# A batched matrix product bound by its transfers: taking out a 64 KB store beside the first loads

## The chip, the core and the metric

The kernel runs on one core of one Trainium2 chip. The time is device microseconds of one execution; medians over several executions are given. The profile is one execution, recorded by the hardware profiler; its "span" runs from the first to the last instruction and is about 2 us shorter than the time.

## The reference

```python
batch, m, k, n = 16, 512, 512, 512
# a: (16, 512, 512) float32 as (batch, k, m);  b: (16, 512, 512) float32 as (batch, k, n)
out = np.matmul(a.transpose(0, 2, 1), b).astype(np.float32)
```

Each of the 16 batches reads 1 MB of a and 1 MB of b and writes 1 MB, some 50.3 MB in all.

## The kernel before

SyncE issues all loads, then all stores. VectorE casts a and b to bf16, TensorE multiplies, ScalarE copies the results from PSUM into one output tile per batch.

```python
NL = 3      # load buffers
NB = 2      # bf16 buffers and PSUM pairs
H = MO // 2
...
o_ts = [pool.tile([P, MO, N], f32, name=f"o{j}") for j in range(batch)]
...
def load(i):
    j = i % NL
    if i >= NL:
        nc.sync.wait_ge(s_acast, i - NL + 2)
    nc.sync.dma_start(a_ts[j][:], a_v[i]).then_inc(s_a[j], 16)
    nc.sync.dma_start(b_ts[j][:], b_v[i]).then_inc(s_b[j], 16)

def store(i):
    if i == 0:
        nc.sync.wait_ge(s_w, 16)
    nc.sync.wait_ge(s_ev1, i + 1)
    nc.sync.dma_start(out_v[i], o_ts[i][:]).then_inc(s_o, 16)

for i in range(batch):
    load(i)
for i in range(batch):
    store(i)
...
nc.gpsimd.memset(o_ts[0][:, 0, 0:P], 0.0).then_inc(s_z, 1)
nc.scalar.wait_ge(s_z, 1)
nc.scalar.dma_start(out_v[0][:, 0, 0:P], o_ts[0][:, 0, 0:P]).then_inc(s_w, 16)
nc.scalar.wait_ge(s_w, 16)
for i in range(batch):
    for h in range(H):
        nc.scalar.wait_ge(s_mm, H * i + h + 1)
        nc.scalar.copy(
            out=o_ts[i][:, 2 * h:2 * h + 2, :], in_=ps_ts[(i % NB) * H + h][:]
        ).then_inc(s_ev1 if h else s_ev0, 1)
```

The four lines with s_z and s_w ahead of ScalarE's loop, and SyncE's wait for s_w in store(0), are the subject. They write 64 KB of zeros, 128 rows of 512 B, into a corner of the output that the first real store overwrites later.

Of the kernel before, what the change touches and what calls it, by code (L numbers as in the profile page):

```python
# [1 line left out]

# [4 lines left out]

@with_exitstack
def kernel(
    ctx: ExitStack,  # L10
    tc: tile.TileContext,
    a: bass.AP,
    b: bass.AP,
    out: bass.AP,
):
    nc = tc.nc
    P = 128
    batch, K, M = a.shape
    _, _, N = b.shape
    KO = K // P  # L20
    MO = M // P
    f32 = mybir.dt.float32
    bf = mybir.dt.bfloat16



    a_v = a.rearrange("bat (ki ko) m -> bat ki ko m", ko=KO)
    b_v = b.rearrange("bat (ki ko) n -> bat ki ko n", ko=KO)
    out_v = out.rearrange("bat (mi mo) n -> bat mi mo n", mo=MO)

    NL = 3
    NB = 2
    H = MO // 2



    pool = ctx.enter_context(tc.tile_pool(name="sb", bufs=1))
    psum = ctx.enter_context(tc.tile_pool(name="ps", bufs=1, space=bass.MemoryType.PSUM))
    a_ts = [pool.tile([P, KO, M], f32, name=f"a{j}") for j in range(NL)]
    b_ts = [pool.tile([P, KO, N], f32, name=f"b{j}") for j in range(NL)]  # L40
    abf_ts = [pool.tile([P, KO, M], bf, name=f"abf{j}") for j in range(NB)]
    bbf_ts = [pool.tile([P, KO, N], bf, name=f"bbf{j}") for j in range(NB)]
    o_ts = [pool.tile([P, MO, N], f32, name=f"o{j}") for j in range(batch)]
    ps_ts = [psum.tile([P, 2, N], f32, name=f"ps{j}") for j in range(NB * H)]

    s_a = [tc.alloc_semaphore(f"s_a{j}") for j in range(NL)]
    s_b = [tc.alloc_semaphore(f"s_b{j}") for j in range(NL)]
    s_o = tc.alloc_semaphore("s_o")
    s_w = tc.alloc_semaphore("s_w")
    s_z = tc.alloc_semaphore("s_z")  # L50
    s_acast = tc.alloc_semaphore("s_acast")
    s_bcast = tc.alloc_semaphore("s_bcast")
    s_mm = tc.alloc_semaphore("s_mm")
    s_ev0 = tc.alloc_semaphore("s_ev0")
    s_ev1 = tc.alloc_semaphore("s_ev1")

    with tc.tile_critical(no_gpsimd_drain=True):  # L57
# [6 lines that stand above are left out]
            nc.sync.dma_start(b_ts[j][:], b_v[i]).then_inc(s_b[j], 16)  # L64

        def store(i):
            if i == 0:
                nc.sync.wait_ge(s_w, 16)
            nc.sync.wait_ge(s_ev1, i + 1)
            nc.sync.dma_start(out_v[i], o_ts[i][:]).then_inc(s_o, 16)  # L70

# [4 lines that stand above are left out]
        nc.sync.wait_ge(s_o, 16 * batch)  # L76

        for i in range(batch):
            n = 16 * (i // NL + 1)
            if i >= NB:  # L80
                nc.vector.wait_ge(s_mm, H * (i - NB + 1))
            nc.vector.wait_ge(s_a[i % NL], n)
            nc.vector.tensor_copy(out=abf_ts[i % NB][:], in_=a_ts[i % NL][:]).then_inc(s_acast, 1)  # L83
            nc.vector.wait_ge(s_b[i % NL], n)
            nc.vector.tensor_copy(out=bbf_ts[i % NB][:], in_=b_ts[i % NL][:]).then_inc(s_bcast, 1)  # L85

        nc.tensor.sem_inc(s_ev0, 1)
        with nc.tensor.Fori(0, batch // NB):
            for u in range(NB):
                a_m = abf_ts[u][:].rearrange("p ko (mi mo) -> p ko mo mi", mo=MO)  # L90
                nc.tensor.wait_ge(s_bcast, 1).then_inc(s_bcast, -1)


                nc.tensor.wait_ge(s_ev0, 1).then_inc(s_ev0, -1)  # L94
                for mo in range(MO):
                    for ko in range(KO):
                        mm = nc.tensor.matmul(  # L97
                            ps_ts[u * H + mo // 2][:, mo % 2, :],
                            a_m[:, ko, mo, :],
                            bbf_ts[u][:, ko, :],  # L100
                            start=(ko == 0),
                            stop=(ko == KO - 1),
                        )
                    if mo % 2:
                        mm.then_inc(s_mm, 1)


        nc.gpsimd.memset(o_ts[0][:, 0, 0:P], 0.0).then_inc(s_z, 1)  # L108
        nc.scalar.wait_ge(s_z, 1)
        nc.scalar.dma_start(out_v[0][:, 0, 0:P], o_ts[0][:, 0, 0:P]).then_inc(s_w, 16)  # L110
        nc.scalar.wait_ge(s_w, 16)
        for i in range(batch):
            for h in range(H):
                nc.scalar.wait_ge(s_mm, H * i + h + 1)
# [5 lines that stand above are left out]
# [1 line left out]
_INS = ['a', 'b']  # L121
_OUTS = [((16, 512, 512), 'float32')]


# [23 lines left out]
```

## Time and profile before

| before | value | how to read it |
|---|---|---|
| time | 125.76 us, median of 3 | 125.68 to 125.79 |
| span | 123.6 us | one profiled execution |
| TensorE busy | 59.6 us (48%) | no compute engine is near the span |
| VectorE, ScalarE busy | 39.3 and 33.6 us | |
| q1 (all loads and real stores) | 50.33 MB, 97.6% of 16 DMA engines | the bound |
| q10 (the small store) | 0.07 MB, 0.2% | what the change takes out |

The lines themselves are in the prediction. A page like this one is read from the bottom of its slices: the row "DMA" is full from the second slice to the last but one, so the time is decided by how soon the stream of transfers begins, by what it carries, and by whether it ever pauses.

### The profile page before, as it was taken

The numbers are of one execution on the slowest core, as the hardware profiler recorded it, in microseconds if no ns is written. First come the engines' busy times: TensorE is split into PE (matmuls) and PEld (weight loads), VectorE is DVE, ScalarE is ACT, GpSimd is POOL, SyncE is SP. The second block draws the span as 40 slices with busy tenths as digits, with TensorE's granted clock in tenths as the row PEclk, the third lists the DMA queues.
The fourth block names the chain that finished last, engine by engine and source line by source line (L and its number), as shares of the span: only waits on it lengthen the run. The fifth ranks groups of instructions, "written<-read, shape, count | busy, mean of one in ns | idle before, by whom it ended". The sixth has DMA issues, their size and how long they took to land. (4 is left out here: it accounts for less than half of the span.)

```text
span 123.6 us, 750 instructions
## 1 busy us (share of the span) xinstructions
PE 59.6 (48%) x256; PEld 28.0 (23%) x256; DVE 39.3 (32%) x32; ACT 33.6 (27%) x33; POOL 0.4 (0%) x5
## 2 busy tenths in 40 slices
PE   0007979695865956859659578596500000000000
PEld 0002344252332522424325234243200000000000
DVE  0055345633554356435543464352000000000000
ACT  0000565623425336244263352432600000000000
POOL 1000000000000000000000000000000000000000
PEclk9999999999999999999999999999985555555555
DMA  2999999999999999999999999999999999999993
GB/s 58 414 424 430 424 424 424 424 419 424 424 424 422 416 424 422 422 424 424 419 414 422 422 424 424 424 422 427 424 427 427 432 430 424 427 435 427 427 424 143
DMA packets 7056, 50.40 MB, mean 408 GB/s; under 512 B 784, under 2 KB 912, under 8 KB 912
## 3 DMA queue, kind: packets, MB, share of 16 engines
q1 hardware_dynamic: 6912, 50.33, 97.6%
q10 hardware_dynamic: 144, 0.07, 0.2%
HBM read 33.55 MB, written 16.84 MB: 408 GB/s over the span
## 5 line engine op out<-in xcount | busy, mean ns | idle before, releaser
L97 PE MATMUL ps<-bbf,abf 128*128 128x512 bf16 x256 | 59.6, 387 | 28.7 <-PEq L94 28.7
L115 ACT COPY o<-ps 128x1024 f32<-128x1024 f32 x32 | 32.3, 1013 | 42.0 <-PE ps L97 42.0
L97 PEld LDWEIGHTS ps<-bbf,abf 128*128 128x128 bf16 x256 | 28.0, 114 | 59.8 <-issue 37.6
L83 DVE CAST abf<-a 128x2048 bf16<-128x2048 f32 x16 | 19.6, 1227 | 25.8 <-DMA a<-in_a_dram 25.8
L85 DVE CAST bbf<-b 128x2048 bf16<-128x2048 f32 x16 | 19.6, 1227 | 19.3 <-DMA b<-in_b_dram 19.3
L115 ACT ACT_TABLE_LOAD x1 | 1.3, 1283 | 13.7 <-PE ps L97 13.7
L108 POOL MEMSET o<- 128x128 f32 x1 | 0.2, 205 | 0.5 <-SPq L57 0.5
L132 POOL MEMSET const-bfloat16-1.0<- 128x1 bf16 x1 | 0.1, 102 | 0.0
L132 POOL MEMSET const-uint8-127<- 128x1 uint8 x1 | 0.1, 102 | 0.0
L132 POOL MEMSET const-float32-0.0<- 128x1 f32 x1 | 0.1, 99 | 0.2 <-issue 0.2
L132 POOL MEMSET const-float32-1.0<- 128x1 f32 x1 | 0.1, 99 | 0.0
## 6 DMA issues: line engine op xcount, KB each, us to landing
a<-in_a_dram SPq DMA_DIRECT2D x16, 1024.0 KB, 8.6
b<-in_b_dram SPq DMA_DIRECT2D x16, 1024.0 KB, 10.7
out_dram<-o SPq DMA_DIRECT2D x16, 1024.0 KB, 25.8
out_dram<-o ACTq DMA_DIRECT2D x1, 64.0 KB, 4.9
```

The costliest lines, as they stand in the source:

```text
L83: nc.vector.tensor_copy(out=abf_ts[i % NB][:], in_=a_ts[i % NL][:]).then_inc(s_acast, 1)
L85: nc.vector.tensor_copy(out=bbf_ts[i % NB][:], in_=b_ts[i % NL][:]).then_inc(s_bcast, 1)
L97: mm = nc.tensor.matmul(ps_ts[u * H + mo // 2][:, mo % 2, :], a_m[:, ko, mo, :], bbf_ts[u][:, ko, :], start=(ko == 0), stop=(ko == KO - 1),)
L108: nc.gpsimd.memset(o_ts[0][:, 0, 0:P], 0.0).then_inc(s_z, 1)
L115: nc.scalar.copy(out=o_ts[i][:, 2 * h:2 * h + 2, :], in_=ps_ts[(i % NB) * H + h][:]).then_inc(s_ev1 if h else s_ev0, 1)
L132: nc = _bacc.Bacc("TRN2", target_bir_lowering=False, num_devices=1)
```

## The change

It takes out the small store, its fill, its two semaphores and the waits on them, and leaves everything else.

```diff
-    s_w = tc.alloc_semaphore("s_w")
-    s_z = tc.alloc_semaphore("s_z")
@@ store(i)
-            if i == 0:
-                nc.sync.wait_ge(s_w, 16)
@@ ahead of ScalarE's loop
-        nc.gpsimd.memset(o_ts[0][:, 0, 0:P], 0.0).then_inc(s_z, 1)
-        nc.scalar.wait_ge(s_z, 1)
-        nc.scalar.dma_start(out_v[0][:, 0, 0:P], o_ts[0][:, 0, 0:P]).then_inc(s_w, 16)
-        nc.scalar.wait_ge(s_w, 16)
```

## The prediction

> **What bounds the kernel now.** I read the page first: its span, its slices and its queue table. The columns of the second fence part are forty equal slices of about 3.1 us each.
>
> ```profile
> span 123.6 us, 750 instructions
> ...
> PE   0007979695865956859659578596500000000000
> ...
> ACT  0000565623425336244263352432600000000000
> ...
> DMA  2999999999999999999999999999999999999993
> GB/s 58 414 424 430 424 424 424 424 419 424 424 424 422 416 424 422 422 424 424 419 414 422 422 424 424 424 422 427 424 427 427 432 430 424 427 435 427 427 424 143
> ...
> q1 hardware_dynamic: 6912, 50.33, 97.6%
> q10 hardware_dynamic: 144, 0.07, 0.2%
> ```
>
> The row "DMA" stands at 9 in every slice but the first and the last, and the rate beneath it is flat at about 424 GB/s. The compute engines are empty in the last eleven slices or so. The main queue q1 carries 50.33 MB; at 0.424 MB per us that is 118.7 us, of a span of 123.6 us. Nothing else on the page is near that. The small store is all that runs on q10: 144 packets, 0.07 MB.
>
> Second, the chain of waits. It follows compute only, so here it must be read as a warning: it ends where ScalarE ends.
>
> ```profile
> 84.62 3.63 PE ps L97 x16
> ...
> 88.28 1.01 ACT o L115
> ```
>
> The last computed tile is ready at 88.28 + 1.01 = 89.3 us, and the span goes on for 34 us with transfers alone. The loads come first in SyncE's program and the stores after them, so compute feeds stores that are queued well ahead. The end of the span is the end of one continuous stream of transfers, and I treat the time as: start of the stream, plus what the stream has to move, plus a tail.
>
> Third, the timeline of the first 20 us, for where the small store stands (start us, duration us, engine, line).
>
> ```profile
> 0.94 0.38 SPq L63 DMA_DIRECT2D a<-in_a_dram  x1
> 0.94 0.20 POOL L108 MEMSET o<- 128x128 f32 x1 [0.50 <-SPq L57]
> 1.18 0.37 ACTq L110 DMA_DIRECT2D out_dram<-o  x1
> 1.38 0.43 SPq L64 DMA_DIRECT2D b<-in_b_dram  x1
> ...
> 5.98 1.23 DVE L83 CAST abf<-a 128x2048 bf16<-128x2048 f32 x1 [5.98 <-DMA a<-in_a_dram]
> ...
> 13.70 1.28 ACT L115 ACT_TABLE_LOAD   x1 [13.70 <-PE ps L97]
> ```
>
> The small store is issued from ScalarE's queue 0.24 us after the first load. ScalarE's first real work begins at 13.70 us and is released by a matmul.
>
> Fourth, the same start in windows of half a microsecond, and the queue table of the first 10 us (columns of a window line: stretch, length, busy time of PE, PEld, DVE, ACT and POOL, TensorE clock, DMA share, GB/s).
>
> ```profile
> 2.00:2.50 0.50, 0.00 (x0) 0.00 (x0) 0.00 (x0) 0.00 (x0) 0.00 (x0) 1.00 1.05 147
> 2.50:3.00 0.50, 0.00 (x0) 0.00 (x0) 0.00 (x0) 0.00 (x0) 0.00 (x0) 1.00 0.40 131
> ...
> 5.00:5.50 0.50, 0.00 (x0) 0.00 (x0) 0.00 (x0) 0.00 (x0) 0.00 (x0) 1.00 0.87 334
> 5.50:6.00 0.50, 0.00 (x0) 0.00 (x0) 0.02 (x1) 0.00 (x0) 0.00 (x0) 1.00 1.15 464
> ```
>
> ```profile
> q10 hardware_dynamic: 144, 0.07, 2.2%
> ...
> out_dram<-o ACTq DMA_DIRECT2D x1, 64.0 KB, 4.9
> ```
>
> The last line says that the small store lands 4.9 us after its issue, so at about 1.18 + 4.9 = 6.1 us. The window lines show a slow ramp of the stream before 3 us, and a short dip in 5.0 to 5.5 us, where most of the small store's packets ran.
>
> **What the Trainium skill says.** "DMA: Bandwidth & Descriptors", section "Issuing engines are not separate DMA queues": transfers from the scalar, sync and gpsimd queues all end up on the same 16 engines and interleave. The trace agrees: the small store has no bandwidth of its own, and the loads' rate dips while it runs. So its bytes are paid from the bounding resource, though it comes from an idle engine.
>
> The same page, section "Queues, rings and completion order": each engine takes turns between the queues that have work, at packet granularity. That fits a store issued second that nevertheless gets through among 6 MB of queued loads, by 6.1 us. It also means that a slow packet of the store could hold up the loads behind it on that engine; in the packet records of the trace no packet of the store is long (27 ns each).
>
> "HBM Reference", section "Specifications (TRN2)": a core streaming alone measures about 425 GB/s, bounded by its 16 DMA engines. The 424 GB/s of this trace agrees. There is no hidden slack in the stream that an earlier start of compute could use.
>
> **The change part by part.**
>
> 1. The small store's packets go. Page: 0.2% of the time of 16 engines, which is too coarse. The first-10-us view: 2.2% of 10 us, so 0.22 us of every engine. The packet records say the same: 128 packets of 27 ns and 16 completion packets of 9 ns are 3.6 us, over 16 engines 0.225 us. A third reading: in 5.0 to 6.0 us the mean rate is (334 + 464) / 2 = 399 GB/s, of which the store is 0.066 MB, so the loads moved about 0.333 MB where a full microsecond gives them 0.427; the lack, 0.094 MB, is 0.22 us. All of it is on the path, since the stream has no gap later in which to make it up: minus 0.22 us.
>
> 2. The fill on GpSimd goes (one MEMSET, 0.20 us at 0.94 us). GpSimd does nothing afterwards. Off the path: 0.
>
> 3. ScalarE's waits and its issue go. ScalarE becomes free for its first copy at about 1 us instead of 6.1 us, but that copy waits for a matmul until 13.70 us. 7.6 us of slack: 0. The table load, 1.28 us, is still at the first copy unless its place moves; even if it moved, only copies would start earlier, and those are not on the path.
>
> 4. SyncE's wait ahead of the first real store goes. Its condition is true from 6.1 us; the first real store is issued at about 72.9 us, behind the last loads. 66 us of slack: 0.
>
> 5. The first batch arrives earlier. b of batch 0 and all after it can land about 0.2 us sooner, and casts and later loads follow. This is the same 0.22 us of item 1 seen from another place and is not added again.
>
> 6. Competition at the start. The ramp before 3 us moves 147 and 131 GB/s where 424 is the stream's rate. The small store is issued inside this ramp. Most of a ramp must be latency of the first reads, but if part of it is the second queue getting in the way, removing it would give more. From the ramp's first packet at about 1.9 us to 4.0 us the stream moves (82 + 147 + 131 + 279 + 475) x 0.5 / 1000 = 0.557 MB (window rates from 1.5 to 4.0 us), which is 1.3 us worth at full rate; so some 0.8 us is lost altogether. I choose to credit 0.04 us, one chance in twenty of it all. That is judgement and no measurement.
>
> Sum: 125.76 - 0.22 - 0.04 = 125.50 us. The median of before is used as base; the 2.2 us between span and median are taken as unchanged.
>
> **The rivals.**
>
> *The small store warms something up.* Somebody put it there on purpose, with a name that suggests warming, so a first write to the output may cost once, and be paid beside the first loads where it is cheap. Without it, the cost would come at the turn from loads to stores. For it: the store needed 4.9 us to land and its packets start only at about 4.5 us, 3.3 us after the issue, while the first load's packets start about 0.95 us after its issue at 0.94. So up to 3.3 - 0.95 = 2.35 us of it could be a cold start. Against it: its packets are of even length; waiting behind loads explains the delay as well; the real stores use SyncE's queue, which the loads have long been using, and they are issued some 20 us before their data moves, so a cost in preparing them would be hidden. If paid in full, 125.5 + 2.35 = 127.9 us, 1.7% slower; a more ordinary size, like the first reads' excess of about 1 us (longest first packet 1.34 us against 0.31 later), gives 126.5 us.
>
> *The ramp is the small store's doing.* Then the stream gains up to 0.8 us more: 125.54 - 0.8 = 124.7 us. For it: the issue falls in the ramp. Against it: its packets run after the ramp is over.
>
> *Hidden anyway.* If the tail of the sixteen engines is set by one whose end is not moved by the store, the 0.22 us vanish and the time stays at 125.76. Against it: every engine has 8 of the 128 packets.
>
> *An engine becomes the bound.* Earlier loads press on the casts: VectorE is busy 39.3 us and TensorE 59.6 us of 123.6. No; it would need three or two times the work.
>
> **Range and chances.** The four ways give 124.7, 125.5, 125.8 and 126.5 us, and the far end of warming 127.9. Weights by judgement: removal of the packets alone, or hidden, 80%; ramp 6%; some warming cost 14%, mostly about 1 us or less. The runs of before scatter by only 0.1 us. The range from 124.9 to 126.0 us holds the first group and some of each neighbour. Two per cent are 2.5 us: to be slower by that, the time must pass 128.3, beyond the far end of the warming rival; to be faster by that, it must be under 123.2 us, which needs 2.3 us beyond item 1 where the whole ramp holds 0.8. So: faster 1%, within 2% 96%, slower 3%.
>
> **What would show each step right or wrong.** In the changed profile, q10 is gone, the packets fall from 7056 to 6912, and the span is about 123.4 us. The rate in 5 to 6 us has no dip (items 1 and 5). The ramp windows 2.0 to 3.0 us still show some 140 GB/s; if they rise, item 6 was the larger one. ScalarE's first copy still starts at about 13.5 to 13.7 us, released by the matmul (item 3). The first real store's issue is still at about 72.7 us (item 4). At the turn from loads to stores, about 80 us, the rate stays at 424: a slice there well below it, or a longer packet, would speak for warming, and so would a span above 124 us. The prediction is wrong if the time falls outside 124.9 to 126.0, or if it lies inside with a dip at the turn and a gain at the start that cancel.

## The result, and the profile after

| | before | after |
|---|---|---|
| time, median of 6 | 125.78 us (125.68 to 125.85) | 125.44 us (125.35 to 125.61) |
| ratio, 95% interval | | 0.9976 (0.9963 to 0.9988) |

The ratio is the mean time of one kernel's runs over that of the other's runs of the same rounds, so it is not quite the ratio of the medians quoted. The gain is about 0.3 us, real and far under 2%.

From the page after, with the same rows as were shown of before:

```profile
span 123.6 us, 744 instructions
...
DMA  3999999999999999999999999999999999999992
GB/s 69 424 427 430 424 424 422 422 422 424 422 422 422 422 422 419 424 422 422 424 419 419 424 419 424 424 424 424 427 427 432 427 427 427 427 427 424 430 427 106
...
q1 hardware_dynamic: 6912, 50.33, 97.7%
```

The queue q10 is gone and q1 is what it was. The span is printed as 123.6 us for both. That is chance: the profiled execution took 125.57 us, one of the slowest of its six, whose spans run from 123.3 to 123.6, and the profiled one of before took 125.61 us, under its median. A difference of 0.3 us must not be read from one pair of spans.

The first 20 us after, and the end of the chain of waits (start us, duration us):

```profile
0.90 1.28 ACT L106 ACT_TABLE_LOAD   x1 [0.90 <-SPq L55]
0.94 0.38 SPq L61 DMA_DIRECT2D a<-in_a_dram  x1
...
5.81 1.23 DVE L79 CAST abf<-a 128x2048 bf16<-128x2048 f32 x1 [5.81 <-DMA a<-in_a_dram]
8.30 1.23 DVE L81 CAST bbf<-b 128x2048 bf16<-128x2048 f32 x1 [1.26 <-DMA b<-in_b_dram]
...
13.43 1.02 ACT L106 COPY o<-ps 128x1024 f32<-128x1024 f32 x1 [11.25 <-PE ps L93]
```

```profile
84.44 3.63 PE ps L93 x16
...
88.09 1.01 ACT o L106
```

Here the gain shows better than in the span: the first cast starts at 5.81 us instead of 5.98, and the last copy at 88.09 instead of 88.28. It is won in the first microseconds and carried to the end. ScalarE's table load has moved to the start of the kernel, because no wait stands in front of it any more; in the run keep_waits below, which keeps one wait there, it still starts at 13.43 us.

The ramp, in the windows of half a microsecond; first before, then after (columns as in the prediction: the last two are DMA share and GB/s; the other windows of before are in the prediction):

```profile
3.00:3.50 0.50, 0.00 (x0) 0.00 (x0) 0.00 (x0) 0.00 (x0) 0.00 (x0) 1.00 0.67 279
```

```profile
2.00:2.50 0.50, 0.00 (x0) 0.00 (x0) 0.00 (x0) 0.18 (x1) 0.00 (x0) 1.00 1.28 180
2.50:3.00 0.50, 0.00 (x0) 0.00 (x0) 0.00 (x0) 0.00 (x0) 0.00 (x0) 1.00 0.39 131
3.00:3.50 0.50, 0.00 (x0) 0.00 (x0) 0.00 (x0) 0.00 (x0) 0.00 (x0) 1.00 0.89 377
...
5.00:5.50 0.50, 0.00 (x0) 0.00 (x0) 0.00 (x0) 0.00 (x0) 0.00 (x0) 1.00 0.98 410
5.50:6.00 0.50, 0.00 (x0) 0.00 (x0) 0.19 (x1) 0.00 (x0) 0.00 (x0) 1.00 0.93 393
```

The stream gets up to rate sooner: 377 GB/s in 3.0 to 3.5 us against 279. That is before the first packet of the small store would have run (4.58 us in the trace of before). In 5 to 6 us the mean rate is 401 GB/s against 399 before, but before a part of that microsecond's work was the small store (107 of its 128 packets, 0.055 MB).

For differences this small, one view of the page is too coarse, and I counted in the trace's packet records. Two of these counts serve below: how many load packets (8 KB each) have started by 4.5 us, and when the 512th of them has ended.

| kernel | store at the start | load packets started by 4.5 us | 512th packet ended, us |
|---|---|---|---|
| before | 64 KB | 92 | 13.06 |
| after, three traces | none | 98, 98, 98 | 12.76, 12.77, 12.71 |

Six packets of 0.31 us over 16 engines are 0.12 us, lost before the store's own packets. With those packets' 0.225 us that makes 0.34 us; the mean of the three 512th packets after is 12.75, so the lead is 0.31 us.

The same can be followed through the whole stream. Take the 6144 packets of 8 KB (loads, then real stores) in the order of their ends, sixteen to a round, and compare the mean end of each round with that of the three traces after. These three agree with each other within 0.03 us from the second round to the last of 384. The trace of before is 0.12 us behind in rounds 2 to 4, all ended ahead of the store's first packet. It is 0.31 us behind from round 9, when the store has run, and still 0.30 at the last round. So the ramp holds 0.12 us of this lag and the store's own packets 0.19. There is one trace of before; in the traces with no small store in the first microseconds, rounds 2 to 4 lie between 0.01 us ahead and 0.08 behind. The times of the three traces after (125.57, 125.29 and 125.25 us) differ by more than their rounds, because the very last packet ends at 121.77, 121.60 and 121.53 us.

### The profile page after: what moved, and what is told of

Its sections match the earlier page's. It is cut to its first block, busy times and chain, and to the rows that moved or that the text cites. A ratio compares the mean times of both kernels' runs of the same rounds, so it can differ in the third digit from the quotient of the medians.

```text
span 123.6 us, 744 instructions
## 1 busy us (share of the span) xinstructions
PE 59.6 (48%) x256; PEld 28.1 (23%) x256; DVE 39.3 (32%) x32; ACT 33.7 (27%) x33; POOL 0.2 (0%) x4
```

## The experiments

Theory P, that of the prediction: the store costs its packets, because they run in the stream that bounds the kernel. Rival W: it warms something, and the removal gives that up. Rival R: a part of its price is paid in the ramp at the start. Each call ran on its own chip with its own runs of before.

### after_again, after_third: the changed kernel once more

No edit.

> The changed kernel unaltered, as the yardstick for the other runs on this chip. Theory P (the price of the store is its packets, 0.22 us of the bounding stream): 0.2 us under the kernel before, ratio about 0.998. Rival W (the store also warms something, a benefit that the removal gives up) would need the price to be above what is measured here; by itself this run cannot tell.

> The changed kernel unaltered, as the yardstick of this call and a third reading of the size of the change: 0.2 to 0.4 us under before, ratio 0.997 to 0.998.

Measured: 125.37 us against 125.77 (ratio 0.9967, interval 0.9954 to 0.9980), and 125.28 us against 125.70 (0.9971, 0.9957 to 0.9985). With the first reading the gain in medians is 0.34, 0.40 and 0.42 us. In medians that is a little more than P's 0.22 us each time; the intervals of the three ratios allow 0.15 to 0.47, 0.25 to 0.58 and 0.18 to 0.54 us, so a single call does not tell the two apart well.

### keep_waits: the fill and a wait stay, the store goes

```diff
         nc.gpsimd.memset(o_ts[0][:, 0, 0:P], 0.0).then_inc(s_z, 1)
         nc.scalar.wait_ge(s_z, 1)
-        nc.scalar.dma_start(out_v[0][:, 0, 0:P], o_ts[0][:, 0, 0:P]).then_inc(s_w, 16)
-        nc.scalar.wait_ge(s_w, 16)
         (SyncE's wait for s_w in store(0) goes too)
```

> The fill on GpSimd, its semaphore and ScalarE's wait for it stay, only the store and the waits on its landing are gone. P: all of the gain comes from the packets, so the time equals the changed kernel's within 0.1 us (0.2 us under before). If instructions and waits were what cost, the time would stay at that of before, 125.8 us.

Measured: 125.44 us beside 125.37 of the changed kernel and 125.77 of before; ratio to before 0.9979 (0.9966 to 0.9992). By 4.5 us 100 load packets had started. The fill and ScalarE's wait for it cost nothing that can be seen; the gain comes with the transfer. What the other two waits cost is not separated here, but the trace of before shows both fulfilled long before they were needed.

### eight: eight small stores

```diff
-        nc.scalar.dma_start(out_v[0][:, 0, 0:P], o_ts[0][:, 0, 0:P]).then_inc(s_w, 16)
-        nc.scalar.wait_ge(s_w, 16)
+        for t in range(8):
+            nc.scalar.dma_start(
+                out_v[0][:, t // 4, (t % 4) * P:(t % 4 + 1) * P], o_ts[0][:, 0, 0:P]
+            ).then_inc(s_w, 16)
+        nc.scalar.wait_ge(s_w, 128)
         (SyncE's wait for s_w in store(0) asks for 128 too)
```

> Eight small stores of 64 KB in 512 B packets, to eight different places of batch 0, in place of one. P: 8 times 0.225 us above the changed kernel, 127.2 us; the step from none to one (measured before) and a seventh of the step from one to eight are the same. W: the first store gives a fixed benefit, so from one to eight the slope is clearly steeper than from none to one. R (the ramp at the start is slowed once by a second queue): from none to one the step is larger than a seventh of the step from one to eight.

Measured: 132.71 us (131.98 to 133.46), ratio 1.0564. None of the theories had said so. The timeline of this run, then its windows:

```profile
24.98 1.93 ACT L118 COPY o<-ps 128x1024 f32<-128x1024 f32 x2 [9.58 <-DMA out_dram<-o]
...
31.43 1.23 DVE L83 CAST abf<-a 128x2048 bf16<-128x2048 f32 x1 [10.72 <-PE ps L97]
...
32.69 0.33 SPq L63 DMA_DIRECT2D a<-in_a_dram  x1
```

```profile
28.00:30.00 2.00, 2.00 (x8) 0.74 (x6) 0.00 (x0) 0.29 (x1) 0.00 (x0) 0.62 0.50 209
30.00:32.00 2.00, 2.00 (x11) 1.07 (x10) 0.56 (x1) 1.29 (x2) 0.00 (x0) 1.00 0.00 0
32.00:34.00 2.00, 2.00 (x11) 1.02 (x9) 1.80 (x2) 1.29 (x2) 0.00 (x0) 1.00 0.44 61
```

This was a fault of my experiment, and a useful one. ScalarE waits for all eight stores to land, and their last completion comes at 24.4 us, as they take turns with the loads. Its copies start at 24.98 us instead of 15.00, TensorE stops, since the program has it wait for the copies before it overwrites PSUM, the casts wait 10.72 us for it, SyncE cannot issue the next loads until 32.69 us, and the stream stands still from 30 to 32 us. The wait that has 7.6 us of slack with one store is what sets the end with eight. The run says nothing about the price of packets.

### eight_free: the same, without the wait

```diff
+    z_t = pool.tile([P, P], f32, name="z")
...
-        nc.gpsimd.memset(o_ts[0][:, 0, 0:P], 0.0).then_inc(s_z, 1)
+        nc.gpsimd.memset(z_t[:], 0.0).then_inc(s_z, 1)
         (eight stores as in "eight", from z_t[:])
-        nc.scalar.wait_ge(s_w, 128)
```

> The eight small stores of the run 'eight', but from a tile of their own, so that ScalarE need not wait for them (that wait lasted until 24.4 us there and stopped the copies). P: without the wait only the packets are left, 8 times 0.225 us above the changed kernel, 127.2 us, and there is no gap in the stream around 30 us. If the eight stores did more to the stream than their packets, the time stays well above that, up to the 132.7 us of 'eight'.

Measured: 126.91 us (126.90 to 127.22), 1.63 us above the changed kernel of the same call. The gap is gone. Each of the eight costs 0.20 us, near P's 0.225. The first costs more than the rest: from none to one it is 0.42 us, from one to eight (126.91 - 125.70) / 7 = 0.17 us each. That has the sign of R, not of W, but the section on eight_late shows another reason for the small slope. By 4.5 us only 83 load packets had started (82 in "eight"), before the first small packet ran at 4.76 us. In rounds 2 to 4 of the packets, the run is 0.28 us behind the changed kernel (0.25 in "eight"), where one small store made it 0.12.

### late: one small store in the middle

```diff
         (no store at the start; in ScalarE's loop, after the copies)
+            if i == 4:
+                nc.scalar.wait_ge(s_ev1, 1)
+                nc.scalar.dma_start(out_v[0][:, 0, 0:P], o_ts[0][:, 0, 0:P]).then_inc(s_w, 16)
```

> One small store of the same 64 KB, but issued by ScalarE in the middle of the loads (after the copies of batch 4, some 35 us in) with real data. P: the packets cost the same 0.22 us wherever they run in the stream, so the time is that of before, 125.7 us, and the ramp in the first 4 us is that of the changed kernel. R: a store away from the start costs less, so the time is that of the changed kernel, 125.45 us.

Measured: 125.50 us, between the changed kernel's 125.37 and before's 125.77; ratio to before 0.9987 (0.9974 to 1.0000). The median lies between the two expectations, and the interval does not exclude P's. The trace places it better: its rounds of packets are 0.03 us behind those of the changed kernel until the store and 0.18 after it, so the store cost 0.15 us. The trace also showed something I had not looked for. From about 16 us on, load packets take 313.5 ns on average in the kernels with one small store or none; up to then, after the ramp, and in the stores at the end, they take 309.0. In this run they fall back to 309.0 ns when the small store has run at 36.8 to 39.5 us, and stay there until about 41 us. Some 4.5 us at 4.5 ns in 309 is 0.07 us given back, so the store should cost 0.225 - 0.07 = 0.16 us; the medians say 0.13 and the rounds 0.15. In the kernel before, the rise comes about 1.3 us later than after the change, worth 1.3 x 4.5 / 309 = 0.02 us.

### eight_late: eight small stores, none at the start

```diff
         (no store at the start; z_t as in "eight_free"; after ScalarE's copies)
+            if 2 <= i < 10:
+                t = i - 2
+                nc.scalar.dma_start(
+                    out_v[0][:, t // 4, (t % 4) * P:(t % 4 + 1) * P], z_t[:]
+                ).then_inc(s_w, 16)
```

> The same eight small stores, none at the start: one after ScalarE's copies of each of batches 2 to 9. P: the packets cost the same wherever they run, 127.2 us. R: if a part of the price belongs to the start, this is cheaper than 'eight_free'. In the run 'late' the load packets went from 313.5 back to 309.0 ns for some 4 us after the small store, worth 4 x 4.5 / 309 = 0.06 us; eight of those are 0.5 us, so on that reading this comes to 126.7 us.

Measured: 126.66 us (126.51 to 126.71), 1.38 us above the changed kernel. From 26 to 66 us load packets averaged 309.8 ns instead of 313.5, so by estimate 40 x 3.7 / 309 = 0.48 us came back of the eight times 0.225 = 1.80 us, which leaves 1.32. The sum of the time of all 8 KB packets, loads and real stores, over 16 engines, fell by 0.36 us, from 120.06 to 119.70, which leaves 1.44; the medians' 1.38 lies between, and in the rounds of the trace the lag grows by 1.13, from 0.09 to 1.22 us. So packets cost about their 27 ns in the middle of the stream too, and the loads give a part of it back. The same return is hidden in eight_free: there the load packets stay at 309.0 ns until about 35 us, some 18 us longer than in before, worth 18 x 4.5 / 309 = 0.26 us. So the small slope from one to eight is no proof of R; the lag ahead of the first small packet is the better sign. In none of these runs was the store worth it: the return is smaller than the price.

### tiny_start: 8 KB at the start

```diff
-        nc.scalar.dma_start(out_v[0][:, 0, 0:P], o_ts[0][:, 0, 0:P]).then_inc(s_w, 16)
-        nc.scalar.wait_ge(s_w, 16)
+        nc.scalar.dma_start(out_v[0][0:16, 0, 0:P], z_t[0:16, :]).then_inc(s_w, 16)
         (z_t and its fill as in "eight_free")
```

> The small store at the start cut to 8 KB (16 partitions x 512 B, one packet for each engine), from a tile of its own and without ScalarE's wait. Its packets cost only 0.04 us. In the traces so far the kernel before had started 92 load packets by 4.5 us, before the first packet of its small store, where the kernels without an early store had started 97 to 100: some 6 packets of 0.31 us over 16 engines, 0.12 us lost in the ramp. If the mere issue from a second queue inside the ramp does that, this run too has about 92 by 4.5 us, and lies 0.12 + 0.04 us above the changed kernel, 125.5 us. If it is the 128 descriptors of the 64 KB, it has 97 to 100 and lies at the changed kernel's 125.3 to 125.4 us. The difference is near the limit of the clock, so the count of packets decides.

Measured: 125.60 us (125.27 to 125.65), before 125.79, ratio 0.9982. The count was 96 by 4.5 us and the 512th packet ended at 12.70 us, as early as in kernels without a store (12.66 to 12.84 us). By the test set beforehand, the count, the mere issue does not slow the ramp; rounds 2 to 6 are 0.02 us ahead of the changed kernel's and those after 0.02 behind, which is the 0.04 us of its packets. But the profiled execution was the 125.27 one, the fastest of six, and the median lies nearer the other expectation. Clock and count contradict each other, and this call has no run of the changed kernel. (The kernels without an early store span 95 to 100 packets; the expectation's 97 to 100 left out late with 96 and eight_late with 95.) Whether the mere issue from a second queue slows the ramp stays open.

### b0_on_act: the first load of b from ScalarE's queue

```diff
-            nc.sync.dma_start(b_ts[j][:], b_v[i]).then_inc(s_b[j], 16)
+            if i > 0:
+                nc.sync.dma_start(b_ts[j][:], b_v[i]).then_inc(s_b[j], 16)
...
+        nc.scalar.dma_start(b_ts[0][:], b_v[0]).then_inc(s_b[0], 16)
```

> The changed kernel, with the first load of b issued from ScalarE's queue beside the first load of a. R: a second queue at the start harms the ramp, so the time rises above the changed kernel's 125.45 us by up to 0.8 us and the rate in 2 to 4 us falls. Opposite view: the ramp is the latency of one queue's first descriptors and a second queue fills it, 0.2 to 0.5 us faster, 125.1 us, which would beat both kernels. P: the ramp is the first reads' latency, no change, within 0.1 us.

Measured: 125.57 us against before 125.73; ratio 0.9989 (0.9976 to 1.0003). It does not beat the changed kernel. The two loads share the engines, so a lands late and the first cast starts at 8.57 us; 97 packets had started by 4.5 us. From round 3 on its trace is 0.06 to 0.08 us behind the changed kernel's. A second queue does not fill the ramp.

### cold_warm: is a first write dearer?

Four small stores, one by one, before any load: two from ScalarE's queue, two from SyncE's.

```diff
         (no wait in store(0); ahead of SyncE's loads)
+        nc.sync.wait_ge(s_w, 32)
+        nc.sync.dma_start(out_v[0][:, 0, 2 * P:3 * P], o_ts[0][:, 0, 0:P]).then_inc(s_w, 16)
+        nc.sync.wait_ge(s_w, 48)
+        nc.sync.dma_start(out_v[0][:, 0, 3 * P:4 * P], o_ts[0][:, 0, 0:P]).then_inc(s_w, 16)
+        nc.sync.wait_ge(s_w, 64)
         for i in range(batch):
             load(i)
...
         nc.scalar.wait_ge(s_w, 16)
+        nc.scalar.dma_start(out_v[0][:, 0, P:2 * P], o_ts[0][:, 0, 0:P]).then_inc(s_w, 16)
+        nc.scalar.wait_ge(s_w, 64)
```

> Four small stores one after the other, each alone on the chip, before any load: two from ScalarE's queue, then two from SyncE's. It is slow on purpose. P: issue to landing is the same for all four within 0.3 us, some 2 us each, so the whole is about 8 us above before; then a first write has no price of its own and the 4.9 us that the store needed beside the loads were waiting behind them. W: the first store takes 1 to 2.35 us longer than the second (and perhaps the third longer than the fourth, if each queue is cold).

Measured: 132.47 us, 6.74 us above before, where P had said about 8. The timeline of this run:

```profile
1.18 0.38 ACTq L113 DMA_DIRECT2D out_dram<-o  x1
2.92 0.34 ACTq L115 DMA_DIRECT2D out_dram<-o  x1
4.64 0.38 SPq L71 DMA_DIRECT2D out_dram<-o  x1
6.39 0.34 SPq L73 DMA_DIRECT2D out_dram<-o  x1
8.09 0.34 SPq L63 DMA_DIRECT2D a<-in_a_dram  x1
```

Each waits for the one before, and the steps are 1.74, 1.72, 1.75 and 1.70 us. The first write of the program costs what the fourth costs, and the first from SyncE's queue what the second does. W is gone: no first write is dearer here. The 4.9 us that the store takes in the kernel before is 1.7 us of its own and 3.2 us beside the loads.

### eight_wide: the bytes of eight, in long packets

```diff
-        nc.gpsimd.memset(o_ts[0][:, 0, 0:P], 0.0).then_inc(s_z, 1)
+        nc.gpsimd.memset(o_ts[0][:, 0:2, :], 0.0).then_inc(s_z, 1)
...
-        nc.scalar.dma_start(out_v[0][:, 0, 0:P], o_ts[0][:, 0, 0:P]).then_inc(s_w, 16)
+        nc.scalar.dma_start(out_v[0][:, 0:2, :], o_ts[0][:, 0:2, :]).then_inc(s_w, 16)
```

> The bytes of the eight small stores (512 KB) in one store of long packets (4 KB rows). If bytes set the price: 0.52 MB at 0.424 MB per us is 1.24 us above the changed kernel, 126.7 us. If the number of packets set it (27 ns each, 128 of them as in one small store), it would cost only 0.2 to 0.3 us, 125.7 us. For 512 B packets the records give 27 ns against 309/16 = 19 ns for the same bytes in a long packet, so P expects some 30% less than for the eight narrow ones. The fill of 1024 columns delays the issue to some 3 us, which should not matter.

Measured: 127.31 us, 1.58 us above its own before, so some 1.9 us above a kernel without a store (1.90 in the rounds of its trace), dearer than the eight narrow ones. The 128 packets of 159 ns are 1.27 us of every engine, as the bytes had said. The rest is in the loads: between 4 and 8 us their packets averaged up to 432 ns (6 to 7 us), which sums to 0.55 us over 16 engines. It is not that they ran beside the store's packets. The store was issued at 1.92 us (not 3, as expected), its first packet ran at 6.28 us, and the loads had grown longer from about 4.5 us on. All load packets that started from 8 to 10.85 us, beside most of the store's packets, took 309 ns. Two windows show it:

```profile
4.50:5.00 0.50, 0.00 (x0) 0.00 (x0) 0.00 (x0) 0.00 (x0) 0.00 (x0) 1.00 0.85 328
...
8.00:10.00 2.00, 0.00 (x0) 0.00 (x0) 0.00 (x0) 0.00 (x0) 0.00 (x0) 1.00 1.03 430
```

P's price of the bytes was right; what P left out is a loss that begins before the store's own packets move, as the 0.12 us does in the kernel before. What causes it is not shown.

### ticks: twelve tiny stores

```diff
         (no store at the start; z_t as in "eight_free"; SyncE's wait in store(0) asks for 192)
+            if 2 <= i < 14:
+                t = i - 2
+                nc.scalar.dma_start(
+                    out_v[0][0:16, t // 4, (t % 4) * P:(t % 4 + 1) * P], z_t[0:16, :]
+                ).then_inc(s_w, 16)
```

> A side question, and a try at beating both: twelve tiny stores (16 partitions x 512 B, one packet for each engine, 8 KB), one after each of batches 2 to 13. Their packets cost 12 x (27 + 9) ns = 0.43 us. If any store sets the load packets back from 313.5 to 309 ns for 4 us, twelve of them give back 12 x 0.06 = 0.7 us, and the time is 125.1 us, under both kernels. If the relief was the work of the 64 KB or chance, the time is 125.4 + 0.4 = 125.8 us.

Measured: 127.70 us, ratio 1.0155. SyncE's own waits in this run name the reason (waiting line, releaser: us in total, times, longest):

```profile
SPq L71 <- DMA out_dram<-z: 10.2, 1, 10.2
```

SyncE's wait ahead of the first real store asks for all twelve, and the last is issued at 78.4 us. The first real store went out at 82.98 us instead of 72.6 in the changed kernel, and the stream thinned at the turn to 224 GB/s in one slice. Again a wait that costs nothing in the kernel before was made to bind. Of the question itself the trace tells this much: load packets averaged about 312.4 ns, so one 512 B packet per engine relieves far less than eight, and over the loads the rounds fell behind the changed kernel's by 0.19 us, from 0.05 to 0.24, of the 0.43 priced. So the stores cost more than they gave back. No version was found that beats the changed kernel.

## Why the prediction was right

The range 124.9 to 126.0 us held 125.44, and the direction and class were right. The range also holds the time of before, so lying in it says little; the gain does more: 0.26 us was forecast, and the medians say 0.34. By its own steps:

1. **The packets, 0.22 us.** Right, if a little high: 0.19 us in the rounds of the trace of before. Eight stores free of waits cost 0.20 us each, and eight late ones 0.17, with part given back by the loads. The step's third reading agreed by chance. It took 427 GB/s as the rate of 5 to 6 us without a store, where the three traces after have 401, 410 and 426, and it counted all of the store's packets, of which 21 ran before 5.0 us.
2. **The fill, 0.** Shown by keep_waits, 125.44 beside 125.37 us.
3. **ScalarE's slack, 0.** Right: the first copy starts at 13.43 us, still released by a matmul. The table load did move, from 13.70 to 0.90 us, which the step had left open; in keep_waits it stays late and the time is the same. The experiment "eight" shows what the slack was worth, by using it up.
4. **SyncE's gate, 0.** Right; "ticks" shows the same gate with its slack used up.
5. **Earlier arrival.** As said: the cast of the first b is 0.21 us earlier (8.30 us instead of 8.51), the last copy 0.19.
6. **The ramp, credited with 0.04 us.** Undersized. The packet counts put it at 0.12 us (92 packets against 98), as do rounds 2 to 4, and three traces with 64 KB or more in narrow packets from the second queue at the very start have 92, 83 and 82, those without such a store 95 to 100. With 0.02 us less for the later rise of the load packets, 0.225 + 0.12 - 0.02 = 0.32 us stands against 0.30 in the rounds of packets and gains of 0.34, 0.40 and 0.42 us in the medians. The step argued that the store's packets run after the ramp; what comes before its packets also counted, and how is not shown. (A hint: SyncE takes 0.87 us to issue its fourth load in before, 0.83 and 0.84 in eight and eight_free, and 0.61 to 0.79 in the others that begin with loads; cause or effect, no run tells.) One execution per kernel carries these counts, and tiny_start did not settle what in the issue does it.

Of the rivals, warming fell to cold_warm and to the result itself. (Its far end was built on 0.95 and 3.3 us from issue to first packet, where the trace has 1.01 and 3.40; and the first real store's data moved about 9 us after its issue, not 20. Nothing hangs on either.) "Hidden anyway" fell: the 512th load packet is 0.31 us earlier and the gain is there. The ramp rival was true at about a seventh of its largest size (0.12 of 0.8 us), so far as one trace of before tells. No engine became the bound except where an experiment made it wait.

One of the signs to look for was badly chosen: a span of 123.4 us in the profile. One execution scatters by as much as the effect. The median of the six spans is 123.4. Two more signs were too coarse: the ramp windows from 2.0 to 3.0 us, 139 GB/s before, have means of 156, 139 and 99 GB/s in the three traces after, and a half-microsecond dip such as that at 5.0 us comes without any store too (361 GB/s in after_third, 311 in keep_waits). The others held: the first real store is issued at 72.65 us, and at the turn, from 75 to 85 us, the rate is 421 and 424 GB/s.

## What to carry to other kernels

Where the row of transfers is full, price a transfer by its packets' time over the 16 engines, whichever idle engine issues it, as a first estimate. In these runs 0.225 us of packets cost between 0.15 (late) and about 0.3 us (at the start), and 1.27 us of them (eight_wide) some 1.9. A wait that costs nothing has a slack that can be read off the timeline: write that number down, since the same wait costs microseconds once the thing waited for grows past it. For effects of a few tenths of a microsecond, compare the time at which the same packet or tile comes in both traces rather than the spans.

## What the Trainium skill lacked or had wrong

- "DMA: Bandwidth & Descriptors", section "Why small descriptors are slow (HBM only)": worked out from its fixed overhead of about 3 cycles per packet, an estimate for a 512 B descriptor (512 / 32 + 3 = 19 cycles for 16) makes it 19% dearer; one more cycle for the 32 bytes of metadata, which the section also names, makes it 25%. Here such a store packet is recorded with 27 ns against 309 / 16 = 19.3 ns for the same bytes in an 8 KB load packet, 40% more. But the 128 of them held the stream up by only 0.19 us (rounds 4 to 9 of the trace of before), 0.19 x 16 / 128 = 24 ns each, 23% more, which is near the estimate. So no error of the page is shown.
- The same page, section "Latency and other measured facts": it gives about 600 ns to the first byte on this path, but not from when that counts. Here the first load's first packet began 1.01 us after the start of its issue and 0.63 us after the end of it (0.94, 1.32 and 1.95 us); for the first store of cold_warm it was 0.88 and 0.50 us.
- The same page, section "Queues, rings and completion order", tells that queues take turns, but not that a store that has been issued can cost the loads something before its own packets move. Here the trace of before is 0.12 us behind the changed kernel's ahead of the store's first packet, and in eight_wide load packets grew from 309 to as much as 432 ns on average, beginning 1.7 us ahead of the store's first packet; once most of the store's packets ran, they were back at 309.
- No page that I read has the drift of the load packets from 309.0 to 313.5 ns, 12 to 15 us after the first of them, nor their return to 309.0 for a few microseconds after a small store. Its cause is open; in 66 us of loads it makes about 66 x 4.5 / 309 = 1.0 us.
